# Two PSUM tiles for the convolution's chunks, rotary embedding from PSUM, K=64 scores and a sink column, in a two-layer hybrid decoder trunk

## The chip, the cores and the metric

One core of one Trainium2 chip runs the whole program once per execution. The metric is the device time of one execution in microseconds; the time before is the median of three runs.

## The reference

The input is x (256 tokens by 1024, float32). Each of two layers does, with RMSNorm ahead of every block:

```
h = h + 1/2 * SwiGLU_1(RMSNorm(h))                 # D_FF 2816
u = RMSNorm(h); [q | k | v | a | g] = u @ W_in      # 512 | 128 | 128 | 512 | 512
  A: attention, window 128, 8 heads of 64 on 2 key/value heads,
     rotary embedding on the first 16 of each head's 64, a learned sink per head in the softmax
  B: a * sigmoid(g) -> causal depthwise convolution, 31 taps -> LayerNorm -> swish
h = h + W_out @ concat(RMSNorm_A(attn), RMSNorm_B(conv))
h = h + 1/2 * SwiGLU_2(RMSNorm(h))
h = h + sigmoid(h @ W_gate) * RMSNorm(p[i] @ W_ple)
```

The sink adds exp(sink - m) to the softmax's denominator and nothing to its numerator. The output is RMSNorm(h).

## The kernel before

Tokens lie in two tiles t of 128. The large products (feed-forward, input projection, gate, convolution half of the output projection) split each float32 operand into a rounded part hi and a rest lo and add three fp32r products: `triple`, through `mms` (L210). ScalarE makes hi (L167) and VectorE lo (L132), on GpSimd for a few units. Scores, probabilities times values, the attention half of the output projection and the embedding of p run in plain float32, where the trace shows two matmul instructions for each `T.matmul`.

PSUM has eight banks of 128x512 float32 in three tags: `bank` (two), `abank` (four), `tbank` (two, for transposes). A tile waits for a free buffer of its tag, and the tags are handed out in the order of the program. All work of the engines is put in order at compile time by a list scheduler that models times; only TensorE's order in the stage ends and in the mixer's tail is that of the program (`ordered()`).

The mixer stage runs the items of `ORDER`: c0 (projection and convolution of channels 0 to 255 as two chunks c of 128), k, q, c1 (channels 256 to 511), u (loads the weights of p), s0 and s1 (scores and softmax of the two query blocks b), x (a table preload), v0 and v1 (probabilities times values), p0 to p3 (embedding of p into an `abank`, then squared and copied by ScalarE), o0 and o1 (normalization by the denominator). Then `TAIL` does the output projection: a.. is the attention half, s. the LayerNorm statistics from the convolution's result y (L736, L738), t. the swish, b. the convolution half.

The convolution gives its first 12 or 13 taps to ScalarE (multiply, L550 and L553) and GpSimd (add, L557), and the rest to VectorE, one instruction for each tap and chunk (L563, L565), in `abank`; at the end y = acc + yp (L567). All this has a lower priority by 600 (`CONV_LATER`).

`scores(b)` multiplies each of four query groups with keys that are padded to 128 rows with zeros (`kTz`), so one product with K=128 gives both key/value heads. VectorE adds the mask and takes the row maximum into m (L630, a custom instruction and a read of its accumulator), then makes nm = -m (L634) and es = sink - m (L636). ScalarE takes exp(es) (L637) and exp of the scores with their row sums den (L643). VectorE adds es to den (L645) and inverts it (L646). `values` transposes the probabilities (L661), copies them out of PSUM (L665, L667) and multiplies. `rope` works on a copy in SBUF that ScalarE has scaled with the RMSNorm factor (L581, L597), in four VectorE instructions (L785 to L788).

Of the kernel before, what the change touches and what calls it, by code (L numbers as in the profile page):

```python
# [19 lines left out]
P = 128  # L20
# [55 lines left out]
def hybrid_trunk_kernel(  # L76
# [338 lines left out]
    cos2 = [cp.tile([P, 16], F32, name=f"cos{t}") for t in range(2)]  # L415
    sin2 = [cp.tile([P, 16], F32, name=f"sin{t}") for t in range(2)]
# [33 lines left out]
    kTz = cp.tile([P, NKV, 256], F32, name="kT")  # L450
# [5 lines left out]
    def mixer_consts():  # L456
        GP.memset(masks[0], 0.0)
        GP.affine_select(masks[0], masks[0], pattern=[[-1, 128]], compare_op=ALU.is_ge, fill=NEG,
                         base=0, channel_multiplier=1)
        GP.memset(masks[1], 0.0)  # L460
        GP.affine_select(masks[1], masks[1], pattern=[[1, 256]], compare_op=ALU.is_gt, fill=NEG,
                         base=0, channel_multiplier=-1)
        GP.affine_select(masks[1], masks[1], pattern=[[-1, 256]], compare_op=ALU.is_ge, fill=NEG,
                         base=128, channel_multiplier=1)
        for e in range(2):
            GP.memset(uT[e][:, :, 0:CW - 1], 0.0)
        GP.memset(kTz, 0.0)
# [20 lines left out]
    def mixer_stage(l, PT, EMB):  # L488
        w = w_in[l]
        X, r, r8 = [None] * 2, [None] * 2, [None] * 2  # L490
        CI, CV = [None, None], []

        def enter(t, b):
# [19 lines left out]
        def rest(nxt):  # L513
            mixer(l, w, X, r, r8, CI, CV, proj, conv_load, PT, EMB, nxt)
# [3 lines left out]
    def mixer(l, w, X, r, r8, CI, CV, proj, conv_load, PT, EMB, nxt):  # L518
# [6 lines left out]
        Y = []  # L525

        def conv_half(e):
# [13 lines left out]
            acc = abank().rearrange("q (c m) -> q c m", c=2)  # L541
            with tc.high_priority(offset=-CONV_LATER):
# [15 lines left out]
                for k in range(np_, CW):  # L558
                    for c in range(2):
                        ws = wconv[l][:, 2 * e + c, k:k + 1]  # L560
                        src = uT[e][:, c, k:k + 256]
                        if k == np_:
                            V.tensor_scalar(out=acc[:, c, :], in0=src, scalar1=ws, scalar2=None, op0=ALU.mult)  # L563
# [11 lines left out]
        def keys_values():  # L575
            ukv.load()
            uq.load({}, QP)
            for t in range(2):
                bkv = proj(ukv, t, 256)
                k_ = wk.tile([P, NKV, HD], F32, tag="k", name="k", bufs=2)  # L580
                S.activation(k_, bkv[:, 0:128].rearrange("q (a b) -> q a b", a=NKV), AF.Copy, scale=r[t])  # L581
# [4 lines left out]
                rope(k_, NKV, t)  # L586
                tb = tbank()
                T.transpose(tb[:, 0:P], k_.rearrange("q a b -> q (a b)"), ident)
                for kv in range(NKV):
                    rs = slice(kv * HD, (kv + 1) * HD)  # L590
                    S.copy(kTz[rs, kv, t * P:(t + 1) * P], tb[rs, 0:P])

        def queries():
            for t in range(2):
                bq = proj(uq, t, 512)
                q_ = wf("q")
                S.activation(q_.rearrange("q (g a d) -> q a g d", g=G, a=NKV),  # L597
                           bq.rearrange("q (a g d) -> q a g d", g=G, a=NKV), AF.Copy, scale=r8[t])
                rope(q_.rearrange("q (n d) -> q n d", d=HD), NH, t)
# [11 lines left out]
        def scores(b):  # L611
            nk = P * (b + 1)
            m = small(NH, "m")
            pr = []
            for gg in range(G):
                sb = bank()
                cs = slice(gg * P, (gg + 1) * P)
                mms(sb[:, 0:NKV * nk], [(qT[b][:, cs], kTz[:, :, 0:nk])])
                if b == 0:
                    if gg % 2 == 0:  # L620
                        sm = wk.tile([P, 512], F32, tag="wr", name="sm", bufs=NWR)
                    pr.append(sm[:, gg % 2 * 256:(gg % 2 + 1) * 256])
                else:
                    if gg == 0:
                        sm = wk.tile([P, G, 512], F32, tag="pr", name="sm", bufs=1)
                    pr.append(sm[:, gg, :])
                for kv in range(NKV):
                    hh = kv * G + gg
                    ks = slice(kv * nk, (kv + 1) * nk)
                    V.tensor_tensor_reduce(out=pr[gg][:, ks], in0=sb[:, ks], in1=masks[b], scale=1.0,  # L630
                                           scalar=sinkb[l][:, hh:hh + 1], op0=ALU.add, op1=ALU.max,
                                           accum_out=m[:, hh:hh + 1])
            nm = small(NH, "nm")
            V.tensor_scalar(out=nm, in0=m, scalar1=-1.0, scalar2=None, op0=ALU.mult)  # L634
            es = small(NH, "es")
            V.tensor_tensor(out=es, in0=sinkb[l], in1=m, op=ALU.subtract)  # L636
            S.activation(es, es, AF.Exp)  # L637
            den = small(NH, "den")
            for gg in range(G):
                for kv in range(NKV):  # L640
                    hh = kv * G + gg
                    ks = slice(kv * nk, (kv + 1) * nk)
                    S.activation(pr[gg][:, ks], pr[gg][:, ks], AF.Exp, bias=nm[:, hh:hh + 1],  # L643
                                 accum_out=den[:, hh:hh + 1])
            V.tensor_tensor(out=den, in0=den, in1=es, op=ALU.add)  # L645
# [7 lines left out]
        def values(b):  # L653
            nk = P * (b + 1)
            pr = PR[b]
            terms = []
            for kc in range(b + 1):
                for kv in range(NKV):
                    tb = tbank()
                    for gg in range(G):  # L660
                        T.transpose(tb[:, gg * P:(gg + 1) * P],  # L661
                                    pr[gg][:, kv * nk + kc * P:kv * nk + (kc + 1) * P], ident)
# [117 lines left out]
    def rope(q, n, t):  # L780
        c3 = cos2[t].unsqueeze(1).to_broadcast([P, n, 16])
        s3 = sin2[t].unsqueeze(1)
        t1 = wk.tile([P, NH, 16], F32, tag="rp1", name="rp1", bufs=2)[:, 0:n, :]
        t2 = wk.tile([P, NH, 16], F32, tag="rp2", name="rp2", bufs=2)[:, 0:n, :]
        V.tensor_tensor(out=t1, in0=q[:, :, 0:16], in1=c3, op=ALU.mult)  # L785
        V.tensor_tensor(out=t2[:, :, 0:8], in0=q[:, :, 8:16], in1=s3[:, :, 0:8].to_broadcast([P, n, 8]), op=ALU.mult)
        V.tensor_tensor(out=t2[:, :, 8:16], in0=q[:, :, 0:8], in1=s3[:, :, 8:16].to_broadcast([P, n, 8]), op=ALU.mult)
        V.tensor_tensor(out=q[:, :, 0:16], in0=t1, in1=t2, op=ALU.add)  # L788
# [174 lines left out]
```

## Time and profile before

| what | value |
|---|---|
| time before, median of 3 runs | 1030.03 us (1029.8 to 1030.08) |
| profiled execution's own time | 1030.14 us |
| its span, first to last instruction | 1028.4 us |
| TensorE busy / weight loads busy | 1000.8 us (97%) / 799.3 us (78%) |
| VectorE, ScalarE, GpSimd busy | 648.1, 560.4, 168.5 us |
| mean granted TensorE clock | 0.992 |

The busy time of TensorE is modelled from starts and ends of pipelined matmuls, so it also counts part of the waiting; a stretch in which it is below the stretch's length has idle time for certain. Of the time, 1.74 us lie outside the span.

### The profile page before, as it was taken

How to read it: one execution, taken by the hardware profiler on the slowest of the kernel's cores; microseconds unless marked ns; L12 is line 12 of the kernel's file. 1: busy time of each engine (PE TensorE's matmuls, PEld its weight loads, DVE VectorE, ACT ScalarE, POOL GpSimd, SP SyncE). 2: the span in 40 equal slices, each digit the busy share in tenths (PEclk: the TensorE clock that was granted, in tenths of full speed). 3: DMA queues.
4: the chain of work that ended last, by engine and by line, in shares of the span. 5: the costliest groups of instructions: out<-in, count | busy, mean ns of one | idle time of the engine just before them, and what ended most of it. 6: DMA issues, size and time to landing. Idle time of an engine off the chain costs nothing.

```text
span 1028.4 us, 13368 instructions
## 1 busy us (share of the span) xinstructions
PE 1000.8 (97%) x4534; PEld 799.3 (78%) x4534; DVE 648.1 (63%) x1100; ACT 560.4 (54%) x1044; POOL 168.5 (16%) x210
## 2 busy tenths in 40 slices
PE   7999999998999999999999999999979999999996
PEld 5888888885568888888888888888835888888886
DVE  6764545789877455555775555457997855555553
ACT  6554444577764444545564445456787545444442
POOL 4400000147623000000000000002765500000001
PEclk9999999999999999999999999999989999999999
DMA  8965656554046655656556565655621566565621
GB/s 270 273 211 164 205 169 207 181 180 130 21 142 194 196 182 187 199 170 204 164 170 206 172 212 169 208 169 174 166 81 61 164 205 200 169 205 166 209 97 41
DMA packets 133396, 177.22 MB, mean 172 GB/s; under 512 B 9184, under 2 KB 109872, under 8 KB 133328
## 3 DMA queue, kind: packets, MB, share of 16 engines
q1 hardware_dynamic: 132144, 174.11, 53.6%
q0 software_dynamic: 1184, 2.27, 0.9%
q8 instruction: 35, 0.57, 0.2%
q14 instruction: 33, 0.27, 0.1%
HBM read 175.29 MB, written 1.05 MB: 171 GB/s over the span
## 4 chain that ended last, share of the span: by engine, by line
PE 92%; DVE 4%; ACT 2%; DMA 1%; POOL 1%; issue 1%; SPq 0%; POOLq 0%; DVEq 0%; ACTq 0%
PE bank L210 61%; PE abank L210 26%; PE tbank L351 2%; PE tbank L305 1%; DMA raw<-in_ffn_w_gate_up_dram 1%; DVE lo L132 1%; ACT sm L643 1%; DVE sm L630 1%; PE tbank L661 0%; PE tbank L482 0%; ACT hi L167 0%; POOL ms_eps L285 0%; DVE pT L665 0%; DVE xl L132 0%; DVE xg L310 0%
## 5 line engine op out<-in xcount | busy, mean ns | idle before, releaser
L132 DVE TENSOR_TENSOR lo<-raw,hi 128x512 fp32r<-128x512 f32 (+1 forms) x519 | 387.0, 791 | 175.0 <-ACT hi L167 168.5
L167 ACT CAST hi<-raw 128x512 fp32r<-128x512 f32 (+1 forms) x544 | 348.1, 689 | 209.7 <-PE abank L210 120.5
L210 PE MATMUL bank<-hi,xh 128*128 128x512 f32 (+1 forms) x904 | 353.1, 391 | 1.4 <-ACT hi L167 1.1
L210 PE MATMUL bank<-hi,xl 128*128 128x512 f32 (+1 forms) x904 | 348.6, 386 | 1.5 <-DVE xl L132 1.5
L210 PE MATMUL bank<-lo,xh 128*128 128x512 f32 (+1 forms) x904 | 348.7, 386 | 0.2
L210 PEld LDWEIGHTS bank<-hi,xl 128*128 128x128 f32 x904 | 170.2, 188 | 37.1 <-DVE xl L132 3.8
L210 PEld LDWEIGHTS bank<-hi,xh 128*128 128x128 f32 x904 | 170.4, 188 | 33.7 <-ACT hi L167 1.5
L210 PEld LDWEIGHTS bank<-lo,xh 128*128 128x128 f32 x904 | 170.5, 189 | 33.3 <-POOL lo L132 0.7
L210 PE MATMUL abank<-hi,hT_hi 128*128 128x512 f32 x352 | 137.7, 391 | 0.0
L210 PE MATMUL abank<-lo,hT_hi 128*128 128x512 f32 x352 | 137.5, 391 | 0.0
L210 PE MATMUL abank<-hi,hT_lo 128*128 128x512 f32 x352 | 137.4, 391 | 0.0
L342 ACT ACTIVATE sg<-bank,r 128x256 f32<-128x256 f32 x88 | 41.7, 474 | 158.3 <-PE bank L210 158.2
L344 DVE SCALAR_TENSOR_TENSOR h<-bank,r,sg 128x256 f32<-128x256 f32 x88 | 42.3, 481 | 130.8 <-ACT sg L342 130.8
L210 PEld LDWEIGHTS abank<-hi,hT_hi 128*128 128x128 f32 x352 | 66.1, 188 | 13.5
L210 PEld LDWEIGHTS abank<-hi,hT_lo 128*128 128x128 f32 x352 | 66.1, 188 | 13.5
L210 PEld LDWEIGHTS abank<-lo,hT_hi 128*128 128x128 f32 x352 | 66.1, 188 | 13.4
L132 POOL TENSOR_TENSOR lo<-raw,hi 128x512 fp32r<-128x512 f32 x25 | 33.1, 1347 | 239.4 <-ACT hi L167 239.4
L565 DVE SCALAR_TENSOR_TENSOR abank<-uT,wconv,abank 128x256 f32<-128x256 f32 x140 | 68.1, 487 | 3.7
L557 POOL TENSOR_TENSOR pp<-pp 128x512 f32<-128x512 f32 x46 | 59.4, 1291 | 44.2 <-ACT pp L553 42.6
L285 POOL TENSOR_SCALAR ms_eps<-ms 128x1 f32<-128x1 f32 x24 | 13.3, 554 | 260.2 <-ACT scratch L292 228.7
L553 ACT ACTIVATE pp<-uT,wconv 128x256 f32<-128x256 f32 x92 | 40.1, 500 | 4.1 <-POOL pp L557 4.1
L132 DVE TENSOR_TENSOR hT_lo<-tbank,hT_hi 128x512 fp32r<-128x512 f32 x44 | 30.4, 692 | 8.2 <-ACT hT_hi L353 5.9
(169 smaller groups left out, 680.0 us busy)
## 6 DMA issues: line engine op xcount, KB each, us to landing
raw<-in_ffn_w_gate_up_dram SPq DMA_DIRECT2D x352, 256.0 KB, 3.9
raw<-in_ffn_w_down_dram SPq DMA_DIRECT2D x88, 512.0 KB, 5.4
raw<-in_w_in_dram SPq DMA_DIRECT2D x32, 256.0 KB, 3.7
raw<-in_w_ple_gate_dram SPq DMA_DIRECT2D x16, 512.0 KB, 4.2
raw<-in_w_in_dram SPq DMA_DIRECT2D x12, 512.0 KB, 4.6
raw<-in_w_out_dram SPq DMA_DIRECT2D x8, 512.0 KB, 4.9
raw<-in_w_out_dram SPq DMA_DIRECT2D x16, 256.0 KB, 5.4
raw<-in_w_ple_dram SPq DMA_DIRECT2D x4, 512.0 KB, 4.9
```

The source lines that it names most:

```text
L132: return eng.tensor_tensor(out=lo, in0=src, in1=hi.bitcast(F32), op=ALU.subtract)
L167: S.copy(hi[:, sl, :], raw[:, sl, :])
L210: T.matmul(dst, a, b, start=first and i == 0, stop=last and i == n - 1)
L285: GP.tensor_scalar(out=e, in0=ms, scalar1=EPS, scalar2=None, op0=ALU.add)
L305: T.transpose(tb[:, i * P:(i + 1) * P], h[t][:, c * P:(c + 1) * P], ident)
L342: S.activation(s, b[:, 0:FC], AF.Silu, scale=r[t])
L344: V.scalar_tensor_tensor(out=o, in0=b[:, FC:2 * FC], scalar=r[t], in1=s, op0=ALU.mult, op1=ALU.mult)
L351: T.transpose(tb[:, k * 256 + t * P:k * 256 + (t + 1) * P], H1[j, t][:, k * P:(k + 1) * P], ident)
L553: S.activation(pp[:, c, :], uT[e][:, c, k:k + 256], AF.Copy, scale=wconv[l][:, ch, k])
L557: GP.tensor_tensor(out=yp, in0=yp, in1=pp, op=ALU.add)
L565: V.scalar_tensor_tensor(out=acc[:, c, :], in0=src, scalar=ws, in1=acc[:, c, :], op0=ALU.mult, op1=ALU.add)
L630: V.tensor_tensor_reduce(out=pr[gg][:, ks], in0=sb[:, ks], in1=masks[b], scale=1.0, scalar=sinkb[l][:, hh:hh + 1], op0=ALU.add, op1=ALU.ma ...
```

## The change

Five edits are made at once.

- The convolution's accumulators: two `abank` tiles are taken at c0, one for each chunk c, and each holds both halves e side by side. Before, each half took one tile with both chunks. The last addition is done per chunk.
- Rotary embedding: `rope` reads the projection in PSUM. The factors cos and sin are scaled with the RMSNorm factor (and 1/8 for queries) beforehand: `rotr`, two ScalarE instructions for each token tile at the stage's entry. VectorE does four instructions with one operand in PSUM, one of them in place in PSUM; ScalarE copies the 48 columns of each head that are not rotated.
- Scores: keys are one 128x256 tile without padding, and each of the two key/value heads is its own product with K=64 on its own half of the partitions, into one `bank` for each head. Block 0 does its 8 products in one go, block 1 in two groups of four, and the maxima of a group come after its products.
- The sink is the first column of each probability tile (129 or 257 columns), copied there by ScalarE, four copies a block, and its exponential comes with the others in den; es, its exponential and the addition go.
- nm = -m is made by ScalarE.

```diff
-            acc = abank().rearrange("q (c m) -> q c m", c=2)
+            if e == 0:
+                ACC.extend(abank() for _ in range(2))
+            acc = [ACC[c][:, e * 256:(e + 1) * 256] for c in range(2)]
...
-                            V.scalar_tensor_tensor(out=acc[:, c, :], in0=src, scalar=ws, in1=acc[:, c, :],
+                            V.scalar_tensor_tensor(out=acc[c], in0=src, scalar=ws, in1=acc[c],
                                                    op0=ALU.mult, op1=ALU.add)
-                V.tensor_tensor(out=y, in0=acc, in1=yp, op=ALU.add)
+                for c in range(2):
+                    V.tensor_tensor(out=y[:, c, :], in0=acc[c], in1=yp[:, c, :], op=ALU.add)
...
+                for i, by in enumerate((r[t], r8[t])):
+                    S.activation(rotr[t][:, i, :], rot[t], AF.Copy, scale=by)
...
-                S.activation(k_, bkv[:, 0:128].rearrange("q (a b) -> q a b", a=NKV), AF.Copy, scale=r[t])
+                rope(k_, bkv[:, 0:128], 1, r[t], rotr[t][:, 0, :])
...
-                for kv in range(NKV):
-                    rs = slice(kv * HD, (kv + 1) * HD)
-                    S.copy(kTz[rs, kv, t * P:(t + 1) * P], tb[rs, 0:P])
+                S.copy(kT[:, t * P:(t + 1) * P], tb[:, 0:P])
...
-                mms(sb[:, 0:NKV * nk], [(qT[b][:, cs], kTz[:, :, 0:nk])])
...
+                S.copy(pr[gg][:, :, 0], sinkb[l].rearrange("q (a g) -> q a g", a=NKV)[:, :, gg])
+            for g0 in range(0, G, per):
+                sb = [bank() for _ in range(NKV)]
+                for g in range(per):
+                    for kv in range(NKV):
+                        rs = slice(kv * HD, (kv + 1) * HD)
+                        T.matmul(sb[kv][:, g * nk:(g + 1) * nk], qT[b][rs, (g0 + g) * P:(g0 + g + 1) * P],
+                                 kT[rs, 0:nk], start=True, stop=True)
+                for g in range(per):
+                    for kv in range(NKV):
+                        hh = kv * G + g0 + g
+                        V.tensor_tensor_reduce(out=pr[g0 + g][:, kv, 1:], in0=sb[kv][:, g * nk:(g + 1) * nk],
+                                               in1=masks[b], scale=1.0, scalar=sinkb[l][:, hh:hh + 1],
+                                               op0=ALU.add, op1=ALU.max, accum_out=m[:, hh:hh + 1])
-            V.tensor_scalar(out=nm, in0=m, scalar1=-1.0, scalar2=None, op0=ALU.mult)
-            es = small(NH, "es")
-            V.tensor_tensor(out=es, in0=sinkb[l], in1=m, op=ALU.subtract)
-            S.activation(es, es, AF.Exp)
+            S.activation(nm, m, AF.Copy, scale=-1.0)
...
-            V.tensor_tensor(out=den, in0=den, in1=es, op=ALU.add)
...
+    def rope(q, src, g, scale, cs):
+        n = NKV * g
+        s4 = src.rearrange("q (a g d) -> q a g d", a=NKV, g=g)
+        s3 = src.rearrange("q (n d) -> q n d", n=n)
+        q4 = q.rearrange("q (g a d) -> q a g d", a=NKV, g=g)
...
+        for i in range(2):
+            V.tensor_tensor(out=t2[:, :, 8 * i:8 * i + 8], in0=s3[:, :, 8 - 8 * i:16 - 8 * i],
+                            in1=cs[:, 16 + 8 * i:24 + 8 * i].unsqueeze(1).to_broadcast([P, n, 8]), op=ALU.mult)
+        S.activation(q4[:, :, :, 16:], s4[:, :, :, 16:], AF.Copy, scale=scale)
+        V.tensor_tensor(out=s3[:, :, 0:16], in0=s3[:, :, 0:16], in1=c3, op=ALU.mult)
+        V.tensor_tensor(out=q4[:, :, :, 0:16], in0=s4[:, :, :, 0:16],
+                        in1=t2.rearrange("q (a g) d -> q a g d", a=NKV), op=ALU.add)
```

## Rows read from the trace of the kernel before

**Rows 1.** Page, part 1: busy us (share of span) xinstructions of each engine.

```profile
PE 1000.8 (97%) x4534; PEld 799.3 (78%) x4534; DVE 648.1 (63%) x1100; ACT 560.4 (54%) x1044; POOL 168.5 (16%) x210
```

**Rows 2.** Windows: length, then busy us of each engine, granted clock, DMA share, GB/s.

```profile
242.00:262.00 20.00, 14.82 (x45) 7.30 (x44) 17.27 (x61) 17.75 (x56) 12.94 (x12) 0.88 0.34 105
...
310.00:450.00 140.00, 140.00 (x634) 115.90 (x633) 80.77 (x115) 68.18 (x112) 7.46 (x6) 1.00 0.59 187
...
745.60:766.00 20.40, 15.00 (x45) 6.90 (x44) 19.08 (x62) 18.03 (x56) 13.35 (x12) 0.91 0.31 101
766.00:789.00 23.00, 22.24 (x77) 11.61 (x76) 17.73 (x36) 15.12 (x35) 16.98 (x24) 0.93 0.15 46
```

**Rows 3.** Chain that ended last, second layer: start us, us on the chain, what.

```profile
746.59 0.26 DVE sm L630
...
750.46 1.22 DVE es L636
...
756.09 0.40 DVE sm L630
...
758.64 0.60 ACT sm L643 x2
...
759.34 2.96 ACT sm L643 x12
...
772.13 4.29 PE abank L210 x10
```

**Rows 4.** Timeline, second layer (PE, DVE), from the last convolution projection's end.

```profile
745.60 0.59 PE L210 MATMUL bank<-kT,qT 128*128 128x256 f32 x2
747.01 0.67 PE L210 MATMUL bank<-kT,qT 128*128 128x256 f32 x2 [0.82 <-DVE m L630]
...
746.78 0.48 DVE L536 SCALAR_TENSOR_TENSOR u<-bank,r,sig 128x256 f32<-128x256 f32 x1
```

**Rows 5.** Timeline, first layer: first score product, last maximum, first exponential of block 1.

```profile
242.12 0.59 PE L210 MATMUL bank<-kT,qT 128*128 128x256 f32 x2
...
254.02 0.48 DVE L630 CUSTOM_DVE_ANT_0 sm<-bank,mask,sink 128x256 f32<-128x256 f32 x1
...
255.75 0.51 ACT L643 ACTIVATE sm<-sm,nm 128x256 f32<-128x256 f32 x1 [1.00 <-DVE es L636]
```

**Rows 6.** Timeline of DVE, first layer: convolution taps in a row, and between other work.

```profile
228.17 5.73 DVE L565 SCALAR_TENSOR_TENSOR abank<-uT,wconv,abank 128x256 f32<-128x256 f32 x11
...
249.33 0.48 DVE L565 SCALAR_TENSOR_TENSOR abank<-uT,wconv,abank 128x256 f32<-128x256 f32 x1
249.72 0.47 DVE L630 CUSTOM_DVE_ANT_0 sm<-bank,mask,sink 128x256 f32<-128x256 f32 x1
```

**Rows 7.** Groups by form, DVE: busy us, mean ns of one, idle before.

```profile
L787 DVE TENSOR_TENSOR rp<-q,sin 128x64 f32<-128x64 f32 x4 | 3.1, 771 | 0.0
...
L636 DVE TENSOR_TENSOR es<-sink,m 128x8 f32<-128x8 f32 x4 | 2.9, 733 | 0.0
...
L645 DVE TENSOR_TENSOR den<-den,es 128x8 f32<-128x8 f32 x4 | 2.5, 634 | 0.0
```

**Rows 8.** Groups by form, ACT.

```profile
L643 ACT ACT_TABLE_LOAD x2 | 2.6, 1283 | 0.0
...
L637 ACT ACTIVATE es<-es 128x8 f32<-128x8 f32 x4 | 0.8, 193 | 0.0
```

**Rows 9.** Timeline, first layer: embedding parts, the first normalization, y and its readers.

```profile
263.19 2.25 PE L210 MATMUL abank<-raw,pinT 128*128 128x512 f32 x4
...
269.55 0.69 DVE L680 TENSOR_TENSOR o<-abank,rT 128x512 f32<-128x512 f32 x1
...
271.66 2.63 POOL L557 TENSOR_TENSOR pp<-pp 128x512 f32<-128x512 f32 x2
...
274.94 0.68 DVE L567 TENSOR_TENSOR y<-abank,pp 128x512 f32<-128x512 f32 x1
...
279.41 1.07 PE L736 MATMUL tbank<-ident,y 128*128 128x128 f32 x8
```

More of the change, by code (lines that the diff above doesn't have):

```diff
@@ L412, in ffn_stage @@
         return Stage(enter, first, rest)
-    cos2 = [cp.tile([P, 16], F32, name=f"cos{t}") for t in range(2)]
-    sin2 = [cp.tile([P, 16], F32, name=f"sin{t}") for t in range(2)]
+    rot = [cp.tile([P, 32], F32, name=f"rot{t}") for t in range(2)]
+    cos2 = [x_[:, 0:16] for x_ in rot]
+    sin2 = [x_[:, 16:32] for x_ in rot]
     def rope_tables():
@@ L449, in hybrid_trunk_kernel @@
     masks = [cp.tile([P, 128 * (b + 1)], F32, name=f"mask{b}") for b in range(2)]
-    kTz = cp.tile([P, NKV, 256], F32, name="kT")
+    kT = cp.tile([P, 256], F32, name="kT")
     vz = [cp.tile([P, NKV, P], F32, name=f"v{t}") for t in range(2)]
@@ L466, in mixer_consts @@
             GP.memset(uT[e][:, :, 0:CW - 1], 0.0)
-        GP.memset(kTz, 0.0)
         for t in range(2):
@@ L491, in mixer_stage @@
         CI, CV = [None, None], []
+        rotr = [wk.tile([P, 2, 32], F32, tag="rotr", name="rotr", bufs=2) for _ in range(2)]
         def enter(t, b):
@@ L513, in rest, with mixer @@
         def rest(nxt):
-            mixer(l, w, X, r, r8, CI, CV, proj, conv_load, PT, EMB, nxt)
+            mixer(l, w, X, r, r8, rotr, CI, CV, proj, conv_load, PT, EMB, nxt)
         return Stage(enter, first, rest)
-    def mixer(l, w, X, r, r8, CI, CV, proj, conv_load, PT, EMB, nxt):
+    def mixer(l, w, X, r, r8, rotr, CI, CV, proj, conv_load, PT, EMB, nxt):
         up = unit_plain(w_ple[l], 0, 2, 0, D, None)
@@ L524, in mixer @@
         cb = gain(l, "cb")
-        Y = []
+        Y, ACC = [], []
         def conv_half(e):
@@ L562, in conv_half @@
                         if k == np_:
-                            V.tensor_scalar(out=acc[:, c, :], in0=src, scalar1=ws, scalar2=None, op0=ALU.mult)
+                            V.tensor_scalar(out=acc[c], in0=src, scalar1=ws, scalar2=None, op0=ALU.mult)
                         else:
-                            V.scalar_tensor_tensor(out=acc[:, c, :], in0=src, scalar=ws, in1=acc[:, c, :],
+                            V.scalar_tensor_tensor(out=acc[c], in0=src, scalar=ws, in1=acc[c],
                                                    op0=ALU.mult, op1=ALU.add)
-                V.tensor_tensor(out=y, in0=acc, in1=yp, op=ALU.add)
+                for c in range(2):
+                    V.tensor_tensor(out=y[:, c, :], in0=acc[c], in1=yp[:, c, :], op=ALU.add)
             Y.append(y)
@@ L579, in keys_values @@
                 bkv = proj(ukv, t, 256)
-                k_ = wk.tile([P, NKV, HD], F32, tag="k", name="k", bufs=2)
-                S.activation(k_, bkv[:, 0:128].rearrange("q (a b) -> q a b", a=NKV), AF.Copy, scale=r[t])
+                k_ = wk.tile([P, P], F32, tag="k", name="k", bufs=2)
+                rope(k_, bkv[:, 0:128], 1, r[t], rotr[t][:, 0, :])
                 for kv in range(NKV):
@@ L596, in queries @@
                 q_ = wf("q")
-                S.activation(q_.rearrange("q (g a d) -> q a g d", g=G, a=NKV),
-                           bq.rearrange("q (a g d) -> q a g d", g=G, a=NKV), AF.Copy, scale=r8[t])
-                rope(q_.rearrange("q (n d) -> q n d", d=HD), NH, t)
+                rope(q_, bq, G, r8[t], rotr[t][:, 1, :])
                 tb = tbank()
@@ L612, in scores @@
             nk = P * (b + 1)
+            per = 512 // nk
             m = small(NH, "m")
             pr = []
-            for gg in range(G):
-                sb = bank()
-                cs = slice(gg * P, (gg + 1) * P)
-                mms(sb[:, 0:NKV * nk], [(qT[b][:, cs], kTz[:, :, 0:nk])])
[L619 to L632, printed above, removed]
+            if b == 0:
+                for _ in range(2):
+                    sm = wk.tile([P, 2, NKV, nk + 1], F32, tag="wr", name="sm", bufs=NWR)
+                    pr += [sm[:, 0], sm[:, 1]]
+            else:
+                sm = wk.tile([P, G, NKV, nk + 1], F32, tag="pr", name="sm", bufs=1)
+                pr = [sm[:, gg] for gg in range(G)]
@@ L653, in values @@
         def values(b):
-            nk = P * (b + 1)
             pr = PR[b]
@@ L661, in values @@
                         T.transpose(tb[:, gg * P:(gg + 1) * P],
-                                    pr[gg][:, kv * nk + kc * P:kv * nk + (kc + 1) * P], ident)
+                                    pr[gg][:, kv, 1 + kc * P:1 + (kc + 1) * P], ident)
                     pT = wk.tile([P, 512], F32, tag="pT", name="pT", bufs=NPT)
@@ L778, in mixer @@
             nxt.first(((HR0, lambda: nxt.enter(1, 0)), (HR1, lambda: nxt.enter(1, 1))))
[L780 to L783, printed above, removed]
-        t2 = wk.tile([P, NH, 16], F32, tag="rp2", name="rp2", bufs=2)[:, 0:n, :]
[L785 to L788, printed above, removed]
+    def rope(q, src, g, scale, cs):
[3 more added lines that the diff above has]
+        q4 = q.rearrange("q (g a d) -> q a g d", a=NKV, g=g)
+        t2 = wk.tile([P, NH, 16], F32, tag="rp2", name="rp2", bufs=2)[:, 0:n, :]
+        c3 = cs[:, 0:16].unsqueeze(1).to_broadcast([P, n, 16])
+        for i in range(2):
[5 more added lines that the diff above has]
+                        in1=t2.rearrange("q (a g) d -> q a g d", a=NKV), op=ALU.add)
     def bcast_row(ap, n, tag="wf", bufs=NWF):
```

6 lines of the change are left out of this document (2 added, 4 removed).

## The prediction

> **What bounds the kernel now.** I read the page's first part to see which engine is the bound: TensorE, busy for 97% of the span, with VectorE at 63% and ScalarE at 54% [rows 1]. So only what shortens TensorE's own work, or a place where it stands still, can move the time. Next the windows, to find such a place. In the feed-forward stretch from 310 to 450 us TensorE is busy without a break; in the 20 us after the last convolution projection it has 14.82 of 20.00 us in the first layer and 15.00 of 20.40 in the second, and in the 23 us after that it is full again to within 0.8 us [rows 2]. So each layer has one hole of about 5 us, where scores and softmax run, and it is in this hole that the change works. The same windows show the granted clock: 0.91 over 20.4 us and 0.93 over 23 us in the second layer mean about 3.7 + 3.2 = 6.9 us at 1.2 GHz instead of 2.4, right behind a stretch in which TensorE had little to do.
>
> Then the chain, to see who fills the hole. It is VectorE (maxima at 0.26 to 0.40 us each, es with 1.22 us) and then ScalarE's exponentials [rows 3]. From the last projection's end to the first exponential of block 1 it is 758.64 - 745.60 = 13.04 us in the second layer and 255.75 - 242.12 = 13.63 us in the first [rows 3 to 5]. After those exponentials the rest of the mixer is TensorE work nearly back to back, so what these 13 us lose or gain should arrive at the end of the layer.
>
> **The change, part by part.**
>
> *Two accumulator tiles.* Taps in a row start every 5.73 / 11 = 0.52 us; a tap with other work behind it lets the next start after 249.72 - 249.33 = 0.39 us [rows 6]. In a row each instruction waits for the one before, since both chunks lie in one tile. With a tile for each chunk the neighbours are independent, so I price a tap at 0.39. A layer has (19 + 18) x 2 = 74 taps: up to 74 x 0.13 = 9.6 us less of VectorE, and 0.2 us more for each y that is split. On the path this is worth nothing: the first half is covered by TensorE's projections until 242.12, the second half's y is ready at 274.94 + 0.68 = 275.6 and TensorE comes for it at 279.41 [rows 9], nearly 4 us later. Nor can y come much sooner, because GpSimd's last sums run until 271.66 + 2.63 = 274.3 [rows 9]. If that cover went, each us of lateness of y would cost a us.
>
> *Rotary embedding.* Query products of 64 columns take 771 ns in the mean [rows 7], far more than their size asks for; these have both operands in SBUF while GpSimd works. With one operand in PSUM, as the convolution's taps have, I expect about 0.25 us each, some 3 us less of VectorE in a layer. All of it lies under projections, so nothing on the path. The projection's bank is held longer, about 1.5 us in place of one ScalarE copy; there are two banks and the next projection that needs it is a whole projection away, so nothing again. ScalarE's non-rotated copy stands between VectorE instructions; behind a waiting one on VectorE stand taps, which have slack. The four `rotr` instructions a layer, about 0.2 us each (as 128x8 takes 0.193 [rows 8]), run at the stage's entry beside the first projection; if ScalarE had no room there they would cost 0.8 us. The single key copy and the missing zeroing of keys are as small and equally covered.
>
> *The sink column.* Eight more ScalarE copies a layer, again near 0.2 us, need only a free tile and fit ahead of the scores. On the path es goes, the sum of den goes, and nm moves: from the last maximum to the first exponential of block 1 it is now 758.64 - 756.49 = 2.15 us in the second layer and 255.75 - (254.02 + 0.48) = 1.25 in the first [rows 3, 5]. Afterwards it is nm on ScalarE, 0.2 us plus two handovers, 0.35 us in all. In front of the queue on ScalarE nm now waits for m; behind it stand convolution products and copies of transposes. For block 0 the table load of 1.28 us [rows 8] then follows nm instead of running beside it, but ScalarE had convolution products to do there anyway.
>
> *K=64.* The trace has no product on half of the partitions. A plain float32 product of 512 columns takes two instructions of 4.29 / 10 = 0.43 us [rows 3]. Upper bound: a K=64 product costs as much for each column as the full one, so a pair for both heads costs what the padded product did, 0.43 us in block 0 and 0.86 in block 1. Lower bound: the two halves of the array work at once, 0.215 and 0.43. Neither row decides, so I take the middle, 0.32 and 0.65, and keep both ends. The Trainium skill, "TensorE: Matmul & The Clock Gate", Part 3 (packing small matmuls), says that matmuls on different row groups run concurrently; by that alone the lower bound would hold and the sum would come out at 1024.4 us. No run here shows it yet.
>
> *The order of scores.* Now a layer's block 0: the second score bank is the one that the last projection occupies, until u is read from it; in the second layer that is at 746.78 behind y and two maxima [rows 4], and without y perhaps 746.8 all told, 1.2 us after 745.60. Then four pairs, 4 x 0.32 = 1.3, a handover 0.1, and eight maxima at 0.28 (0.26 [rows 3] and a handover) = 2.2: 4.8 us. Block 1: two pairs 1.3, four maxima 1.6, the next two pairs of which 0.4 are covered by the last maximum 0.9, four maxima 1.6: 5.4 us. With 0.35 for nm this makes 10.5 us against 13.04 and 13.63: 2.5 + 3.1 = 5.6 us gained. With the upper bound of K=64 it is 11.7, a gain of 3.2; with the lower 9.2, a gain of 8.2.
>
> What goes against it: VectorE now has three gaps a layer, in which the scheduler will put taps of 0.39 us; on average half of one is in the way, 3 x 0.2 x 2 = 1.2 us. And the embedding loses its place. Part p0 runs at 263.19, between products of v1, in the accumulator that the first convolution half gave back [rows 9]; after the change both accumulators stay taken until the last y, so p0 has to wait for o0 to free one, and TensorE loses that cover while probabilities are copied. One such wait is about the 0.69 us of a 128x512 read of PSUM [rows 9], between nothing (other products fill it) and the 1.7 us of p0 itself: 0.7 x 2 = 1.4 us.
>
> **Sum.** 5.6 - 1.2 - 1.4 = 3.0 us less. The profiled execution took 1030.14 us (span 1028.4 and 1.74 outside), 0.11 above the median; 1030.1 - 3.0, given against the median: 1027.0 us.
>
> **Rivals.** *More: pairs run together.* With the lower bound and no lost cover it is 8.2 - 1.2 = 7.0 us: 1023.0. For it: two halves of the array are two different sets of rows. Against: block 0's eight exponentials come first on ScalarE; 4.3 us for its maxima, 0.35, 1.28 for the table and about 3 (six of block 1's take 2.96 [rows 3]) make 8.9 us, so that at 9.2 nothing else may slip.
>
> *Nothing: the gain is given back.* Either the exponentials of block 1 find ScalarE busy with convolution products in front of them, or the hole in TensorE's work, now shorter but emptier, leads to more time at 1.2 GHz. Today one layer has 6.9 us of it; half as much again in one layer costs 1.7 us while TensorE is the bound, in both 3.4. That ends at 1030.4. What speaks for it is that the second layer's slow stretch lies in the products right after the hole [rows 2].
>
> *Slower: accumulators run out.* Four embedding parts of 1.7 us have to pass through the two `abank` tiles of v0 and v1, as long as the convolution holds the other two. If o0 comes as late as now (269.55 [rows 9]), p0 to p3 are pushed to the end, one after the other, each waiting for its predecessor's two ScalarE reads, about 1.3 us: 3 x 1.3 x 2 = 7.8 us. Against 5.6 - 1.2 this gives 1033.5. It decides from the point where TensorE has no other work: the attention half of the output projection (32 instructions of 0.43, 13.8 us a layer) can fill in, but only once o0 is done, so what matters is whether o0 moves ahead of p0. I think it does, since nothing else is ready.
>
> *The tiles change nothing.* If independent taps keep 0.52 us, VectorE is as full as before; since the sum takes nothing from it, the time would still be near 1027.
>
> **How the numbers follow.** The measurement tells apart about 0.2%, 2.1 us: below 1028.0 is faster, above 1032.1 slower. The forecast's case has 0.46 (own range 1024.9 to 1029.0, about a sixth of it above 1028.0), the larger gain 0.16, nothing 0.24, accumulators 0.14. Faster is 0.46 - 0.08 + 0.16 = 0.54, within the bound 0.24 + 0.08 = 0.32, slower 0.14. The range leaves out the far halves of the two outer cases, 1022.5 to 1032.5.
>
> **What the profile after would show.** Taps in a row every 0.39 us; no VectorE instruction of rotary embedding over 0.4 us; K=64 pairs starting within one product's time (concurrent) or two (not); from the last projection to block 1's first exponential about 10.5 us; o0 ahead of p0. The prediction is wrong if that stretch stays at 13 us, if TensorE waits for an `abank` behind v1, or if the time at 1.2 GHz grows by more than 3 us a layer.

## The result, and the profile after

| | before | after |
|---|---|---|
| median of the runs (range) | 1030.05 us (1029.8 to 1030.27) | 1055.22 us (1054.04 to 1057.31) |
| ratio, 95% interval | | 1.0247 [1.0229, 1.0264] |
| span of the profiled execution | 1028.4 us | 1055.5 us |
| mean granted TensorE clock | 0.992 | 0.976 |

The change costs 25 us; the forecast was 3 us less. The page's first part, after:

```profile
PE 1020.0 (97%) x4566; PEld 809.7 (77%) x4566; DVE 625.9 (59%) x1092; ACT 562.5 (53%) x1064; POOL 167.2 (16%) x209
```

VectorE has 22 us less to do than in [rows 1], as meant, and TensorE, the bound, has 19 us more with 32 instructions more. The windows of [rows 2], laid on the same places of the program:

```profile
244.90:264.90 20.00, 16.62 (x56) 9.52 (x56) 18.31 (x65) 17.23 (x55) 13.35 (x12) 0.74 0.34 106
310.00:450.00 140.00, 139.83 (x638) 114.87 (x637) 82.61 (x118) 69.86 (x115) 12.17 (x12) 1.00 0.58 185
760.80:781.20 20.40, 16.49 (x55) 9.76 (x54) 18.37 (x66) 17.66 (x56) 14.27 (x14) 0.67 0.33 104
781.20:804.20 23.00, 16.28 (x36) 7.90 (x37) 5.57 (x13) 11.59 (x27) 9.55 (x8) 0.78 0.00 0
```

The granted clock of the hole fell from 0.88 and 0.91 to 0.74 and 0.67, and the 23 us behind it, once full, now have 16.28 us of work and half the instructions. Their timeline (first layer, all engines, lines of weight loads left out) shows why:

```profile
268.68 6.64 POOL L562 TENSOR_TENSOR pp<-pp 128x512 f32<-128x512 f32 x5 [0.53 <-ACT pp L558]
...
269.97 0.60 PE L676 MATMUL tbank<-ident,rexp 128*128 128x128 f32 x4
...
275.35 0.76 DVE L573 TENSOR_TENSOR y<-abank,pp 128x256 f32<-128x256 f32 x2 [6.33 <-POOL pp L562]
...
275.83 6.67 PE L210 MATMUL abank<-raw,pinT 128*128 128x512 f32 x8 [4.40 <-DVE y L573]
...
279.65 0.60 ACT L821 ACTIVATE scratch<-abank 128x512 bf16<-128x512 f32 x1 [6.07 <-PE abank L210]
...
280.70 0.60 ACT L678 COPY rT<-tbank 128x512 f32<-128x512 f32 x1
281.33 0.69 DVE L680 TENSOR_TENSOR o<-abank,rT 128x512 f32<-128x512 f32 x1 [5.23 <-ACT rT L678]
```

VectorE ended its taps early and stood idle for 6.33 us until GpSimd had added its own. Then came y, and with y the accumulator was free: TensorE stands idle for 4.40 us before p0, waiting for it. o0's transposes had long run (269.97), but their copy rT is queued on ScalarE behind p0's square, so o0 waited for p0, and nothing was left to put in between. The order of the program is `v0 v1 p0 o0 p1 p2 o1 p3`, so p0 asks for its accumulator ahead of o0. In [rows 9] p0 ran at 263.19, inside the work on v1.

The chain through the first layer's hole (from the first score product to block 1's exponentials):

```profile
250.00 1.28 ACT L645
...
251.84 1.25 PE tbank L661 x3
253.09 2.00 PE bank L631 x4
255.09 1.04 PE tbank L661 x4
256.14 2.00 PE bank L631 x4
258.14 0.42 PE tbank L661
...
258.58 0.59 ACT pT L667
259.17 0.81 ACT pp L558 x2
259.97 0.11 ACT nm L640
...
260.10 1.99 ACT sm L645 x7
```

In [rows 3] this chain was VectorE; now TensorE stands in it. Block 0's transposes for v0 (L661), which wait for its exponentials, lie between the pairs of block 1's score products (L631), and a pair takes 2.00 us of the chain there, at the low clock. Two small marks of other edits, from the timelines of TensorE, ScalarE and VectorE:

```profile
219.39 1.70 ACT L558 ACTIVATE pp<-uT,wconv 128x256 f32<-128x256 f32 x4
220.99 0.50 ACT L591 ACTIVATE v<-bank,r 128x64 f32<-128x64 f32 x2
...
221.54 0.50 PE L210 MATMUL bank<-hi,xh 128*128 128x512 f32 x1 [0.90 <-ACT v L591]
...
223.17 4.00 DVE L570 SCALAR_TENSOR_TENSOR abank<-uT,wconv,abank 128x256 f32<-128x256 f32 x10
```

q's first projection waits for a bank whose last readers, the v copies, are queued behind convolution products on ScalarE. Last, the page's groups for the second feed-forward product, of before and then of after:

```profile
L210 PE MATMUL abank<-hi,hT_hi 128*128 128x512 f32 x352 | 137.7, 391 | 0.0
L210 PE MATMUL abank<-lo,hT_hi 128*128 128x512 f32 x352 | 137.5, 391 | 0.0
L210 PE MATMUL abank<-hi,hT_lo 128*128 128x512 f32 x352 | 137.4, 391 | 0.0
```

```profile
L210 PE MATMUL abank<-hi,hT_hi 128*128 128x512 f32 x352 | 140.1, 398 | 0.0
L210 PE MATMUL abank<-lo,hT_hi 128*128 128x512 f32 x352 | 139.0, 395 | 0.0
L210 PE MATMUL abank<-hi,hT_lo 128*128 128x512 f32 x352 | 138.2, 393 | 0.0
```

412.6 us became 417.3 in code that the diff doesn't touch. From one start to the next these matmuls are 0.227 us apart before, and 0.2341, 0.2315 and 0.2296 (in the order of the lines) after, at a granted clock of 1.00.

### The profile page after: what moved, and what is told of

Its sections match the earlier page's. It is cut to its first block, busy times and chain, and to the rows that moved or that the text cites. A ratio compares the mean times of both kernels' runs of the same rounds, so it can differ in the third digit from the quotient of the medians.

```text
span 1055.5 us, 13439 instructions
## 1 busy us (share of the span) xinstructions
PE 1020.0 (97%) x4566; PEld 809.7 (77%) x4566; DVE 625.9 (59%) x1092; ACT 562.5 (53%) x1064; POOL 167.2 (16%) x209
## 4 chain that ended last, share of the span: by engine, by line
PE 91%; ACT 5%; POOL 1%; DVE 1%; DMA 1%; issue 1%; SPq 0%; POOLq 0%; DVEq 0%; ACTq 0%
PE bank L210 60%; PE abank L210 25%; PE tbank L351 2%; ACT pp L558 1%; POOL pp L562 1%; DMA raw<-in_ffn_w_gate_up_dram 1%; PE tbank L305 1%; ACT sm L645 1%; PE bank L631 1%; PE tbank L661 1%; ACT hi L167 1%; PE tbank L482 1%; ACT pp L555 0%; DVE lo L132 0%; ACT pT L667 0%
## 5 line engine op out<-in xcount | busy, mean ns | idle before, releaser
L210 PE MATMUL abank<-hi,hT_hi 128*128 128x512 f32 x352 | 140.1, 398 | 0.0
L570 DVE SCALAR_TENSOR_TENSOR abank<-uT,wconv,abank 128x256 f32<-128x256 f32 x140 | 58.0, 479 | 0.0
```

The source lines that it names most:

```text
L210: T.matmul(dst, a, b, start=first and i == 0, stop=last and i == n - 1)
L570: V.scalar_tensor_tensor(out=acc[c], in0=src, scalar=ws, in1=acc[c], op0=ALU.mult, op1=ALU.add)
```

## The experiments

The landmarks below are from each run's timeline, first and second layer. "Projections": first u transpose to first score product. "exp b1" and "conv rows": from the first score product to block 1's first exponential and to the first product of `conv_rows`. "Hole clock": granted clock from the first score product to the end of block 1's exponentials. Each ratio is to the kernel before on the run's own chip, where its median was 1029.13 to 1030.05 us.

| kernel | us | ratio to before [95%] | projections | exp b1 | conv rows | hole clock |
|---|---|---|---|---|---|---|
| before | 1030.05 | 1 | 29.46, 29.46 | 13.63, 13.04 | 51.14, 51.75 | 0.90, 0.99 |
| after | 1055.22 | 1.0247 [1.0229, 1.0264] | 30.73, 30.74 | 15.20, 15.08 | 59.33, 62.21 | 0.73, 0.65 |
| e1 tiles only | 1043.75 | 1.0142 [1.0127, 1.0157] | 29.43, 29.43 | 15.78, 16.30 | 58.49, 59.02 | 0.91, 0.90 |
| e2 all but tiles | 1040.05 | 1.0106 [1.0089, 1.0123] | 30.69, 30.69 | 14.19, 15.03 | 52.62, 51.65 | 0.69, 0.67 |
| e3 after, o before p | 1041.86 | 1.0122 [1.0107, 1.0137] | 30.70, 30.70 | 15.20, 15.08 | 52.35, 53.80 | 0.73, 0.69 |
| e4 after, fewer GpSimd taps | 1047.23 | 1.0168 [1.0150, 1.0187] | 30.75, 30.72 | 15.21, 15.08 | 55.50, 55.76 | 0.64, 0.64 |
| e6 K=64 only | 1031.76 | 1.0024 [1.0014, 1.0035] | 29.55, 29.55 | 15.57, 14.90 | 52.07, 51.48 | 0.68, 0.64 |
| e7 rotary only | 1032.85 | 1.0031 [1.0017, 1.0045] | 30.58, 30.58 | 14.34, 13.70 | 53.53, 49.57 | 0.90, 0.90 |
| e8 sink, own slots | 1026.24 | 0.9969 [0.9957, 0.9981] | 29.46, 29.46 | 12.84, 12.45 | 49.79, 48.56 | 1.00, 1.00 |
| e11 e8 + rotary, v first | 1024.64 | 0.9948 [0.9933, 0.9963] | 29.42, 29.42 | 12.01, 11.71 | 49.47, 47.48 | 1.00, 1.00 |
| e12 e11 + tiles, o first | 1031.97 | 1.0021 [1.0012, 1.0030] | 29.56, 29.59 | 14.16, 14.14 | 51.95, 52.75 | 0.91, 0.91 |

In the first four expectations A is that the accumulators are what costs, B that the rest of the change is.

**e1: the tiles alone**, put into the kernel before (the lines of the diff with `ACC`, `acc[c]` and the split y). **e2: the changed kernel without them.**

> The kernel before with the two accumulator tiles alone. Theory A (accumulators): both are held until the last y, so the embedding parts p0 to p3 stand behind y, TensorE stands still after v1 and runs the parts in a row, and much of it runs at 1.2 GHz: 1040 to 1052 us, p0 starting after y. Theory B (the hole of the scores itself grew, by batching and K=64, and the clock fell with it): the tiles alone do nothing or save VectorE time, 1027 to 1031 us.

> The changed kernel with the convolution's accumulators as before, so rotary embedding, K=64 scores and sink column alone. Theory A: most of the 25 us goes; what stays is the projection's bank held longer (1.3 us a layer) and the later exponentials of block 1 (about 1.5 us a layer): 1030 to 1038 us. Theory B: 1045 to 1056 us.

e1 shows the new wait of p0 in a kernel that has nothing else of the change (its timeline of VectorE and of TensorE):

```profile
273.05 0.76 DVE L570 TENSOR_TENSOR y<-abank,pp 128x256 f32<-128x256 f32 x2 [3.37 <-POOL pp L559]
...
273.53 8.83 PE L210 MATMUL abank<-raw,pinT 128*128 128x512 f32 x16 [3.55 <-DVE y L570]
```

y is 2 us sooner than before, and conv rows come 7.35 and 7.27 us later: 14.6 us, all that e1 costs. e2 falls between the two expectations: 1.06% remain without the tiles, so the rest of the change costs too.

**e3: o0 and o1 ahead of the p items**, and **e4: eight taps for GpSimd in the second half**, in the changed kernel.

```
e3  ORDER = "c0 k q c1 u s0 s1 x v0 v1 o0 o1 p0 p1 p2 p3"   # was ... v0 v1 p0 o0 p1 p2 o1 p3
e4  POOL_TAPS = (12, 8)          # was (12, 13)
```

> The changed kernel with o0 and o1 ahead of p0 to p3 in the order, nothing else. Theory A: the parts then take the accumulators that o0 and o1 free, and nothing on ScalarE stands behind a square that waits for y: 1035 to 1046 us, p0 starting before y. Theory B: 1052 to 1057 us.

> The changed kernel with 8 instead of 13 taps of the second half on ScalarE and GpSimd, the rest on VectorE. Theory A, with y waiting for GpSimd's sums: five sums of 1.28 us come off GpSimd and 10 products off ScalarE, y and p0 come up to 5 us sooner, 1040 to 1050 us. Theory B: no change within 2 us of 1055.

With o0 ahead in the order (e3's timeline of TensorE), p0 gets o0's accumulator instead of y's and waits 0.31 us:

```profile
270.30 1.98 PE L210 MATMUL abank<-raw,pinT 128*128 128x512 f32 x4 [0.31 <-DVE o L680]
```

13 of the 25 us come back, by one line of order. In e4 y comes 2.6 and 5.0 us sooner after the first score product and p0 still starts right behind it: what p0 waits for is y. In the changed kernel y waits for GpSimd; in e4, with five sums fewer there, it follows VectorE's last taps without a wait.

**e6: the K=64 scores alone** (unpadded kT, products and maxima in groups, softmax as before). **e7: the rotary embedding alone.** **e8: the sink column alone**, with K=128 scores and with slots of its own for block 0's probabilities (the one line by which its probability tiles differ from the changed kernel's):

```diff
-                    sm = wk.tile([P, 2, NKV, nk + 1], F32, tag="wr", name="sm", bufs=NWR)
+                    sm = wk.tile([P, 2, NKV, nk + 1], F32, tag="sm0", name="sm", bufs=2)
```

> The kernel before with the K=64 scores alone (unpadded kT, two or four products into a bank, one bank per key head), old rotary embedding, old softmax, one accumulator tile. Theory serial (two K=64 products of one pair run one after the other): TensorE's time for the scores is that of before, and block 1 has two groups where it had four, so its first exp comes 0.5 to 2 us later than before after the first score product; 1029.5 to 1034 us. Rival (two row groups at once): 64x256 instructions start in pairs under 0.05 us apart, block 1's first exp comes 1 to 3 us earlier, 1024 to 1028.5 us.

> The kernel before with the rotary embedding from PSUM alone. Theory bank (the projection's bank stays held until the v copies that stand behind rope's own copy on ScalarE): TensorE stands still 0.7 to 1.3 us before q's first projection in each layer, and the first u transpose to the first score product takes 30.3 to 30.8 us for 29.46; 1031 to 1033.5 us. Rival (nothing on the path; the 1.27 us of the changed kernel are from its accumulators' taps): 29.4 to 29.7 us, 1028 to 1030.5 us.

> The kernel before with the sink column alone (K=128 scores bank by bank; the negated maximum on ScalarE), block 0's probability tiles in slots of their own so that hT's stay 2048 B apart. Theory gain: last maximum to first exp of block 1 falls from 1.25 and 2.15 us to 0.4 and the exps start 0.8 to 1.7 us sooner in each layer, 1026.5 to 1029 us. Rival (what is saved ahead of exp comes back behind it, or as time at the low granted clock): 1029 to 1031 us. Rival (the 129 and 257 columns cost the maxima and exps more than the four removed instructions): over 1031 us.

e6 and e7 went as their first theories say. e8 is faster, and by a little more than expected, but not by the way its theory has: from the last maximum to block 1's first exponential it takes 1.45 and 1.1 us, not 0.4, as its second layer shows (timelines of VectorE and ScalarE, from the last maximum's end at 755.65):

```profile
755.57 0.08 DVE L630 DVE_READ_ACCUMULATOR2_ANT m<- 128x1 f32 x1
...
756.02 0.56 ACT L661 COPY pT<-tbank 128x512 f32<-128x512 f32 x1
756.48 0.21 ACT L634 ACTIVATE nm<-m 128x8 f32<-128x8 f32 x1
756.72 0.51 ACT L639 ACTIVATE sm<-sm,nm 128x257 f32<-128x257 f32 x1
```

e6's timeline of TensorE has the second and third of block 1's four pairs:

```profile
247.05 1.13 PE L627 MATMUL bank<-kT,qT 64*128 64x256 f32 x4 [0.40 <-DVE m L632]
...
250.33 2.07 PE L627 MATMUL bank<-kT,qT 64*128 64x256 f32 x4
```

The four instructions of the upper pair (two heads, two each) start 0.320, 0.216 and 0.216 us apart in the trace, at the high clock. None starts together with another, and four times 0.216 is the 0.86 us priced for the padded product: the two heads' products are serial. The lower pair ran at 1.2 GHz, 0.427 us apart but for the first gap of 0.589. In all kernels of the table with K=64 the hole's clock is 0.64 to 0.73, in all with K=128 it is 0.90 or more.

In e7 TensorE stands idle for 0.91 us behind the v copies, and the projections take 1.12 us more in each layer. In e8 block 1's exponentials start 0.8 and 0.6 us sooner after the first score product, and in the profiled execution the clock is never lowered in the hole or in the tail (from block 1's exponentials to the first product of `conv_rows`). The windows of hole and tail of each layer, in e8 and then in the kernel before:

```profile
242.20:258.97 16.77, 11.30 (x38) 5.12 (x36) 14.20 (x51) 15.86 (x54) 11.65 (x10) 1.00 0.41 125
258.97:291.97 33.00, 30.92 (x113) 16.52 (x114) 26.06 (x51) 25.42 (x60) 18.61 (x25) 1.00 0.17 49
744.30:760.70 16.40, 11.08 (x38) 5.09 (x36) 14.16 (x51) 15.50 (x51) 11.63 (x10) 1.00 0.41 126
760.70:792.83 32.13, 30.83 (x113) 16.55 (x114) 26.61 (x52) 25.28 (x59) 18.86 (x25) 1.00 0.17 51
```

```profile
242.10:259.80 17.70, 12.97 (x38) 5.83 (x36) 15.24 (x55) 15.57 (x50) 11.68 (x10) 0.90 0.38 118
259.80:293.30 33.50, 32.30 (x114) 17.45 (x114) 26.71 (x53) 25.56 (x60) 18.64 (x25) 0.95 0.16 49
745.60:762.70 17.10, 12.01 (x38) 5.14 (x36) 15.94 (x55) 15.47 (x51) 11.66 (x10) 0.99 0.38 121
762.70:797.35 34.65, 33.58 (x115) 17.85 (x114) 27.64 (x53) 25.45 (x59) 18.66 (x25) 0.91 0.15 47
```

Part of e8's gain is the clock itself. The mean granted clock of an execution was 0.991 to 0.996 in the kernel before on e8's chip and 0.996 to 0.998 in e8. The one execution of each at 0.996 took 1028.17 and 1026.30 us, 1.9 us apart, where the medians are 3.6 us apart.

**The slots: e5, e9, e10 and e13 to e18.** Block 0's probability tiles share four slots (tag "wr") with hT, the stationary operand of the second feed-forward product, and 129 columns for each of two query groups and two heads make a slot 2064 B where it had 2048. Each run but e9 and e16 (which are the changed kernel) is the kernel before with one edit of sizes, such as

```diff
e5 -                        sm = wk.tile([P, 512], F32, tag="wr", name="sm", bufs=NWR)
e5 +                        sm = wk.tile([P, 516], F32, tag="wr", name="sm", bufs=NWR)
e15 -            s = wk.tile([P, FC], F32, tag="sg", name="sg", bufs=NSG)
e15 +            s = wk.tile([P, FC + 8], F32, tag="sg", name="sg", bufs=NSG)[:, 0:FC]
...   (the same for the convolution's tile of this tag)
```

> The kernel before, with one edit: the four slots that block 0's probability tiles share with the feed-forward's hT are 2064 B apart instead of 2048 B; no instruction is added, removed or reshaped. Theory S (the slots): matmuls whose stationary operand is hT start 0.230 to 0.234 us apart instead of 0.227, as in the changed kernel; about 1,056 of them in the first feed-forward stretch and its like elsewhere give +4 to +7 us, so 1033 to 1037 us, with kT to conv rows as before. Rival (the spacing in the changed kernel comes from something else, the clock or the neighbours on other engines): 1028 to 1031 us and 0.227 us.

> The changed kernel with one edit: the four slots that block 0's probability tiles share with hT are 2112 B apart instead of 2064 B (33 times 64 B), the 129-column tiles lie in the first 2064 B. Theory S (where a slot begins sets the spacing, and the growth by 64 B is harmless): matmuls from hT start 0.227 us apart again, 5 to 7 us less than the changed kernel, 1048 to 1050.5 us. Rival (any growth of the slots costs it): 1053.5 to 1057 us with 0.230 to 0.234 us.

> The kernel before with those slots 2080 B apart (65 times 32 B) and nothing else. If only beginnings off a 32 B step cost time: 0.227 us and 1028.5 to 1031 us. If beginnings off a 64 B step do: hT's matmuls at 0.229 to 0.234 us in the slots that begin at 32, and 1031.5 to 1036 us.

> The kernel before with the four slots of hT and block 0's probabilities 2560 B apart (five times 512 B), so that every slot begins a multiple of 512 B behind the first, as with 2048 B. If the beginnings to one another in steps of 512 B (or less) decide: 0.227 us from start to start and 1028.5 to 1031 us. If any distance but 2048 B costs: 0.229 us or more and 1032 to 1037 us.

> The same with 2304 B (nine times 256 B): hT_hi stays at multiples of 512 B behind the first slot, hT_lo lies 256 B off. If steps of 256 B are enough: 0.227 us and 1028.5 to 1031 us. If it takes 512 B: 0.229 us or more where hT_lo comes in, 1031.5 to 1036 us.

> The kernel before with all four slots begun 64 B later and still 2048 B apart (two small tiles ahead of them made 32 B longer). If the slots' phase to the moving operand's tiles, which lie on multiples of 512 B from the first slot of before, decides: 0.229 us or more and 1032 to 1037 us. If only the phase of hT_hi and hT_lo to each other does: 0.227 us and 1028.5 to 1031 us.

> The changed kernel with block 0's probability tiles in slots of their own, hT's 2048 B apart. Theory S: 0.227 us from start to start, 5 to 7 us less than the changed kernel, 1048 to 1050.5 us; what is left against before is the accumulators, the bank behind the v copies and the K=64 scores. Rival (the spacing is a result of what else the changed kernel does there): 1053 to 1057 us.

> The kernel before with all four slots of hT begun 128 B later, still 2048 B apart, the moving operands where they were. If steps of 128 B are enough: 0.227 us and 1028 to 1030.5 us. If it takes 256 B: 0.229 us or more and 1032 to 1037 us.

> The kernel before with every tile of both working pools begun 64 B later, hT's slots and the moving operands hi, lo together (one small constant tile made 64 B longer). If the phase of the stationary to the moving operand decides: all matmuls 0.227 us apart as before and 1028 to 1030.5 us. If the place of the stationary operand in the memory decides: hT's matmuls and also those from xh and xl 0.230 us or more apart, 1040 us or more.

"hT busy" is the sum of the three groups shown above; "phase" is where hT's slots begin against the moving operands' tiles, modulo 256 B, as the sizes give it and as the built programs have the addresses, which no trace prints (2064 is rounded up to 2080 there, so e5 and e10 are one layout).

| kernel | phase of hT's slots, B | hT busy | us | ratio [95%] |
|---|---|---|---|---|
| before | 0 | 412.6 | 1030.05 | 1 |
| e5, 2064 apart | 0, 32, 64, 96 | 417.3 | 1036.07 | 1.0062 [1.0047, 1.0077] |
| e10, 2080 apart | 0, 32, 64, 96 | 417.8 | 1034.96 | 1.0047 [1.0032, 1.0062] |
| e13, 2560 apart | 0 | 412.6 | 1029.27 | 1.0000 [0.9991, 1.0009] |
| e14, 2304 apart | 0 | 412.6 | 1029.52 | 1.0003 [0.9994, 1.0013] |
| e15, all four 64 later | 64 | 418.9 | 1036.15 | 1.0066 [1.0051, 1.0081] |
| e17, all four 128 later | 128 | 418.3 | 1036.01 | 1.0066 [1.0051, 1.0081] |
| e18, hT and moving operands 64 later | 0 | 412.6 | 1029.72 | 1.0003 [0.9993, 1.0012] |
| e9, after, 2112 apart | 0, 64, 128, 192 | 416.6 | 1054.24 | 1.0230 [1.0212, 1.0248] |
| e16, after, own slots | 0 | 412.6 | 1048.71 | 1.0188 [1.0173, 1.0203] |

My first theory, that a slot must begin on a 32 or 64 B step, fell with e9 and e10. The second stands: what counts is the phase of the stationary operand to the moving one, modulo 256 B. Offsets of 256 B (e14) and 512 B (e13) cost nothing, 64 B (e15) and 128 B (e17) do. e15 and e18 have hT at the same addresses; what differs is where the tiles of the weights lie, hi and lo, which these products read, and raw (page groups of e15, then of e18):

```profile
L210 PE MATMUL abank<-hi,hT_hi 128*128 128x512 f32 x352 | 139.8, 397 | 0.0
L210 PE MATMUL abank<-lo,hT_hi 128*128 128x512 f32 x352 | 139.6, 397 | 0.0
L210 PE MATMUL abank<-hi,hT_lo 128*128 128x512 f32 x352 | 139.5, 397 | 0.0
```

```profile
L210 PE MATMUL abank<-hi,hT_hi 128*128 128x512 f32 x352 | 137.7, 391 | 0.0
L210 PE MATMUL abank<-lo,hT_hi 128*128 128x512 f32 x352 | 137.5, 391 | 0.0
L210 PE MATMUL abank<-hi,hT_lo 128*128 128x512 f32 x352 | 137.4, 391 | 0.0
```

Between e15 and e18 the tiles that other engines read and write at the same time moved too, so a part of theirs is not excluded. e16 gives the changed kernel 6.5 us back (1055.22 to 1048.71).

**e11: what is left of the change when its costs are taken out**: e8 and the rotary embedding from PSUM, with the v copies first. **e12: the same with the two tiles and e3's order.** The v copies' place, against the changed kernel:

```diff
-                rope(k_, bkv[:, 0:128], 1, r[t], rotr[t][:, 0, :])
                 for kv in range(NKV):
                     ...
                     S.activation(vz[t][:, kv, cs], src, AF.Copy, scale=r[t])
+                rope(k_, bkv[:, 0:128], 1, r[t], rotr[t][:, 0, :])
```

> The kernel before with the sink column in slots of its own and the rotary embedding from PSUM, with the two v copies issued ahead of rope's instructions. Theory order (the bank was held because the v copies stood behind rope's copy on ScalarE): no stand of TensorE behind v before q's projection, 29.4 to 29.6 us from u transpose to first score product, first exp of block 0 0.7 us sooner than before; 1025 to 1027.5 us, the sink column's own time. Rival (rope itself holds the bank, by its product written back to it): 30.3 us or more and 1028.5 to 1031 us.

> The run before this one with the two accumulator tiles and both attention outputs ahead of the p items in the order. Theory accumulators (p0 needs a tile that y sets free): p0 stands behind both outputs or y, conv rows 2 to 4 us later in each layer, 1028 to 1034 us. Rival (with the order mended the shorter taps are a gain): y 2 to 4 us sooner and under 1025 us.

In e11 q's projection starts right behind the transpose (timeline of TensorE):

```profile
219.16 0.27 PE L591 MATMUL tbank<-ident,k 128*128 128x128 f32 x1
219.19 0.47 PE L210 MATMUL bank<-hi,xh 128*128 128x512 f32 x1
```

Block 0's first exponential comes 6.2 us after the first score product for 6.95. e11 is 0.52% faster than the kernel before and the fastest of all, a little below its expected range; of that, 0.21% is beyond e8, with intervals that just overlap. e12 is 7.3 us slower than e11: with everything else mended the tiles in e3's order still cost, and p0 waits for o0 there. That order without the tiles was not run, so the two are not told apart in e12. Its timeline of TensorE:

```profile
267.65 1.99 PE L210 MATMUL abank<-raw,pinT 128*128 128x512 f32 x4 [0.90 <-DVE o L678]
```

## Why the prediction was wrong

The parts, each alone: tiles +1.42%, slots +0.62, rotary +0.31, K=64 +0.24, sink -0.31: 2.28% together, measured 2.47 [2.29, 2.64]. The 0.19 between them is within the errors of five ratios. Point by point:

- **Accumulators, the step that failed first.** "p0 has to wait for o0 to free one" was priced at 1.4 us; p0 waited for y, and that measured 14.6 us (e1). Taps in a row came at 0.39 us (4.00 us for ten), as priced, and were worth nothing, as said. But tiles are handed out in the order of the program, where p0 stands ahead of o0: it got the convolution's tile and so y's lateness. The prediction itself had GpSimd's end at 274.3, y behind it, and "if that cover went, each us of lateness of y would cost a us"; it did not see that the tiles take the cover away by tying p0 to y. The rival "accumulators run out" had the place and was mis-sized, 7.8 us for 14.6, because it too let p0 wait for o0. "I think it does, since nothing else is ready" (o0 ahead of p0) was half true: its transposes went ahead, its copy on ScalarE did not, for that queue has an order too.
- **Rotary embedding.** The VectorE instructions measured 0.17 to 0.29 us in the mean, near the 0.25 priced, and were hidden. "The next projection that needs it is a whole projection away, so nothing again" failed: 1.27 us a layer in the changed kernel, 1.12 alone, nothing with the v copies first (e11).
- **K=64.** The upper bound held (0.86 us a pair), the middle was taken. The Trainium skill, "TensorE: Matmul & The Clock Gate", Part 3 (Packing small matmuls), says that matmuls on different row groups run concurrently. The traces here do not agree for these float32 products into two banks: in every run with K=64 they start one after the other, 0.216 us apart with 256 columns, so the measurement decides. What the sum missed is the clock, 0.64 to 0.74 through the hole, at which a pair takes 2.07 us to the end of its last product, for 1.13 at the high clock.
- **Order of the scores.** 10.5 us was forecast, 11.7 with serial pairs; 15.20 and 15.08 were measured. Block 0 came out near its price (its last maximum ended at 249.04, 4.1 us after the last projection, for 4.8). Block 1 took 9.95 us (249.04 to 258.99) for 5.4, and the rest, to the exponential at 260.10, 1.1 us for 0.35: transposes that wait for block 0's exponentials stand between the pairs, the pairs run at 1.2 GHz, and VectorE's gaps held 13 taps and a copy rather than half a tap each, in part while it waited for the pairs.
- **Sink column.** nm on ScalarE was priced 0.35 us from the last maximum to the exponential. e8 has 1.45 and 1.1 (maxima end at 253.57 and 755.65, the exponentials start at 255.02 and 756.72): nm stands behind convolution products and a copy in ScalarE's queue. Before it was 1.25 and 2.15, so this gains only in the second layer. In the first the maxima end 1.0 us sooner (11.39 us after the first score product for 12.38), but that is the clock's doing: in the second layer of before, at a clock of 0.99, they end after 10.88 us, sooner than e8's 11.39. At the high clock, then, the exponentials come 0.2 and 0.6 us sooner (12.84 and 12.45 us after the first score product for 13.04). The edit is worth 3.6 us alone (1029.81 to 1026.24 on one chip), part of it as time at the high clock: the tails are 33.0 and 32.1 us at 1.00 for 33.5 and 34.7 at 0.95 and 0.91. Why the clock holds in e8 is not shown.
- **Slots.** No step of the prediction looked at where the tiles lie. It is the second largest cost.
- **Signs named ahead.** All three that would make the prediction wrong came: the stretch stayed above 13 us, TensorE waited for an accumulator behind v1, and the time at 1.2 GHz grew, in the second layer's two windows, from 6.9 us to 20.40 x 0.33 x 2 + 23.00 x 0.22 x 2 = 23.6.

## What to carry to other kernels

Before a buffer is held longer, ask who gets it next in program order and what its last reader waits for: here p0, which had run 12 us before y was ready, was tied to y and so to the slowest engine's last instruction, for 14.6 us. A copy that frees a bank belongs ahead of new work in its engine's queue. When a tile changes size, look at what shares its slots: in this kernel stationary and moving operands had to stay in step modulo 256 B.

## What the runs showed of the hardware

- A matmul of 512 float32r columns starts 0.227 us after the one before when both operands' tiles are in phase modulo 256 B, and 0.233 us after it when the stationary one is 64 or 128 B off (e15, e17): 2.5 to 2.8%, 6 to 7 us over this kernel's 1,056 such products. Weight loads keep 188 ns in the page either way.
- Two float32 products with K=64 on different halves of the partitions, into two banks, take the time of both: with 256 columns their instructions start 0.216 us apart at the high clock and 0.427 us at the low one (e6).
- With K=64 scores TensorE's granted clock in the hole was 0.64 to 0.74 and with K=128 scores 0.88 or more, in every kernel. The two kinds of kernel also differ in the order of the work around the scores; which of the differences goes with the clock was not tried, so the cause stays open.
